# First branch's inverse multiplied into the scan's keys and output scores once per pair, two visits of TensorE per scan step instead of three, and a new order of the woven part

## Chip, cores and metric

The kernel runs on one core of one Trainium2 chip. The metric is device time in microseconds (us) of one execution; the times shown are of several executions of the same program. Names of engines: TensorE (PE in the profile, PEld its weight loads), VectorE (DVE), ScalarE (ACT), GpSimd (POOL), SyncE (SP, which issues most of the DMA).

## What is computed

One layer of a hybrid backbone over 256 latent tokens with a prefix of 256 context tokens, width 2048, in f32. After a modulated norm, one projection feeds two token mixers that run side by side, RWKV-7 time mixing (16 heads of 64) and a chunked gated DeltaNet (8 heads of 128), both in two directions, the context's final state being the start of the latent scan. A gated merge, an output projection and a SwiGLU FFN follow. The part that the change touches is the first mixer's recurrence:

```python
def rwkv7_scan(r, w, k, v, kk, bb, s0):
    def step(s, inp):
        r_t, w_t, k_t, v_t, kk_t, b_t = inp
        sa = jnp.einsum('bhij,bhj->bhi', s, kk_t)
        s = s * w_t[:, :, None, :] - sa[..., None] * b_t[:, :, None, :] + v_t[..., None] * k_t[:, :, None, :]
        return s, jnp.einsum('bhij,bhj->bhi', s, r_t)
    ...
    s_fin, y = lax.scan(step, s0, xs)
    return jnp.moveaxis(y, 0, 1), s_fin
...
out_a = [prefix_scan(rwkv7_scan, rwkv_dir_inputs(fa_c, d), rwkv_dir_inputs(fa, d), s0a, d == 1)
         for d in range(2)]
o_a = rwkv_readout(out_a[0][0] + out_a[1][0], fa, rw_r_k, rw_ln_w, rw_ln_b).astype(h.dtype)
```

## The kernel before

**Stages.** The program runs through a head (modulation, norm, the low-rank projections), a woven part (lines with the helper's line 145: both mixers and all remaining input projections), and then, in plain order, the merge (`pa`, `pb`), the output projection (`wout`), and the FFN (`wgu`, `wdn`). The woven part lies between about 134 and 1310 us of the profiled execution.

**The first mixer in chunks.** Heads go in 8 pairs, two heads of 64 on the two halves of the 128 partitions. The 512 tokens are cut into 8 chunks of 64 (4 of the context, 4 latent), in each of two directions. Per pair, `prepare` makes decayed keys, `grams` makes the chunk matrices (`LT`, the triangular matrix to invert; `LAl`/`LAc`, which carry state and values into the chunk; `Pm`, the output scores; `KB`, the keys token by token that carry the chunk's result into the state). `inverse` calls `invert`, which inverts 16 blocks of 64 and gives two views of the result, plain (`N_`, tile T0) and transposed (`Nt_`, tile Tx); `full` says whether both are made complete. `values` and `scan` follow. The second mixer's `head_inverse` uses the same `invert` with `full` set.

**A scan step.** `scan` takes 8 steps per pair, both directions and both heads at once. In a step TensorE is visited three times, each visit after a copy of the visit before:

1. `la` x `vx` into bank `ps` (four matmuls), then ScalarE copies the result to R1;
2. the inverse `Tt` x R1 into the other half of `ps` (four matmuls); with it go two identity matmuls that put the old state into bank `acc`, and in the latent steps four output matmuls; ScalarE then copies the result over the value rows of `vx`;
3. `KB` x `vx` onto `acc` (the new state), and in the latent steps `Pm` x `vx` (the output). VectorE scales the state by the chunk's decay and writes it into the next `vx`.

**What sets the order.** All woven work is written as generators. `Weave.run` goes through them before the kernel is built and fixes the order of instructions on each engine: it takes the piece that could start first by prices in `Lane` (`cost` of an instruction) and `LAT` (`hop` between engines, `turn` for a change of kind on TensorE, `grp` instructions at a time); among equals the lower rank given to `weave.add` goes first. On the chip each engine works strictly through its list and waits on semaphores. `products` issues the projection matmuls in split form, three f32r matmuls per weight block (`mm<-hxh,whi`, `mm<-hxl,whi`, `mm<-hxh,wlo`), with `cast` making `whi` on ScalarE and `wlo` on VectorE from loads that SyncE issues. 40 of these products are gate columns; `GATES_A` and `GATES_B` say how many of them are free to run beside which pair and which head. PSUM banks are shared out as `pab` (2 banks), `pib` (1), `psb` (2) and `mmb` (3).

Of the kernel before, what the change touches and what calls it, by code (L numbers as in the profile page):

```python
# [11 lines left out]
F32 = mybir.dt.float32  # L12
# [6 lines left out]
P = 128  # L19
# [91 lines left out]
class Lane:  # L111
# [5 lines left out]
    def __getattr__(self, name):  # L117

        def op(out, *a, **k):
# [8 lines left out]
            elif name == "matmul":  # L128
# [3 lines left out]
                elif rows <= 64 and m <= 64:  # L132
                    cost, kind = 0.026 if rows < 64 else max(0.06, 0.05 + 0.00015 * n), (rows, m)
                elif m <= 64:
                    cost, kind = 0.085 if m == 64 else 0.12, (rows, m)
                else:
                    cost = (0.0054 + 0.00167 * n) * (1.22 if rows == 96 else 1)
# [8 lines left out]
        return op  # L146

# [123 lines left out]
def emit(ctx: ExitStack, tc, A, out, dbg=None):  # L271
# [284 lines left out]
    def invert(pool, Lt, parts, nu, which, full, fill):  # L556
# [90 lines left out]
        yield [e.matmul(ps[src, 32 * i:32 * i + 32], qo[dst, i, :], Tx[dst, u, cd], start=True, stop=True)  # L647
               for i, h, u, src, dst, cs, cd in quads]
        for h in range(2):
            yield [out(Tx, d, h, ps, True) for d in range(2)]  # L650
        weave.release(pib)
        if full:
            ps = yield pib
            yield [e.matmul(ps[dst, 32 * i:32 * i + 32], Tx[dst, u, cd], qo[dst, i, :], start=True, stop=True)
                   for i, h, u, src, dst, cs, cd in quads]
            for h in range(2):
                yield [out(T0, d, h, ps, False) for d in range(2)]
            weave.release(pib)
# [59 lines left out]
    def lowrank():  # L718
# [17 lines left out]
        for p in range(NPAIR):  # L736
# [8 lines left out]
            for j in (0, 2, 1, 3):  # L745
                ps = yield psb
                yield e.matmul(ps, w[:96, 4 * (p % 2) + j], lin[:, j], start=True, stop=True)
                weave.add(2, lowrank_out(p, j, ps, out[j]))

    def prepare(p):  # L750
# [78 lines left out]
        if p + 1 < NPAIR:  # L829
            weave.add(10 * p + 13, prepare(p + 1))  # L830

    def grams(p, d):
# [4 lines left out]
        def m4(a, b, rows):  # L837
# [4 lines left out]
        yield [e.matmul(ps[h if src is ic else half[1 - j], 64 * c:64 * c + 64], src[h, T + 64 * c:T + 64 * c + 64],  # L842
                             lc[h, c, j, :], start=True, stop=True)
                    for c in range(4) for ps, src in ((p1, ic), (p2, kt)) for j, h in enumerate(half)]
# [7 lines left out]
        yield [e.matmul(ps[h if src is ic else half[1 - j], P * c:P * c + P], src[h, 64 * c:64 * c + 64], la[h, c, j, :],  # L852
                             start=True, stop=True) for c in range(4) for ps, src in ((p1, ic), (p2, kt)) for j, h in enumerate(half)]
# [23 lines left out]
    def inverse(p):  # L877
# [6 lines left out]
        _, o["Tt"], _ = yield from invert(rs, lambda h, u: LT[64 * h:64 * h + 64, u // 8, u % 8, :],  # L884
# [855 lines left out]
```

## Time and profile before

| what | us |
|---|---|
| median of 3 runs | 2293.3 |
| lowest, highest | 2292.33, 2308.79 |
| profiled execution: span from first to last instruction | 2286.3 |
| woven part in it | 134 to 1310 |
| of it the eight scans | 280 to 810 |
| merge and output projection | 1310 to 1560 |
| FFN | 1560 to 2286 |

The profiled execution gives a span only; its distance to the median of the runs (7.0 us) is what lies around the first and last instruction, plus the difference between runs. In the profile's rows a group reads: line, engine, operation, tiles out<-in, shapes, xcount | busy us, mean ns of one | idle time of the engine before them and what ended it. A window reads: stretch and its length, then busy us and (xcount) of PE, PEld, DVE, ACT, POOL, then the granted TensorE clock, the DMA share and GB/s. A wait reads: who waited <- for whom: us in total, times, the longest. A timeline row reads: start, us until the end of the merged instructions, engine, line, operation, tiles, forms, count. An f32 matmul of the program shows as two matmul instructions in the trace, an f32r matmul as one.

### The profile page before, as it was taken

Reading aid. Unit: us, or ns where it says so; the run is one execution under the profiler, and the core shown is the slowest. Engines: PE = TensorE matmul, PEld = TensorE weight load, DVE = VectorE, ACT = ScalarE, POOL = GpSimd, SP = SyncE. Lnnn points to the kernel's source line nnn. Section 1 sums busy time; section 2 is a strip of 40 time slices with the busy share of each in tenths; the row PEclk is TensorE's granted clock in tenths of the full one; section 3 lists DMA queues with packets and bytes.
Section 4 is the critical chain, followed back from the end, with each engine's and each line's share of the span. In section 5 each row is a group of like instructions: output and inputs, shape, how many; then the busy total and the mean of one; then the engine's idle time right before and its main releaser. Section 6 shows DMA issues by size and latency. Waiting matters only on the chain. (4 is left out here: it accounts for less than half of the span.)

```text
span 2286.3 us, 54678 instructions
## 1 busy us (share of the span) xinstructions
PE 2184.5 (96%) x22904; PEld 1925.0 (84%) x22904; DVE 1561.3 (68%) x3225; ACT 1056.6 (46%) x1922; POOL 110.3 (5%) x185
## 2 busy tenths in 40 slices
PE   7998999999999999999999989899999999999998
PEld 4766577777777788888888889889999999999997
DVE  3446588888877586899997668774656656444444
ACT  3245554544555554444453445444444444444443
POOL 0000000000000010111110040000000000000000
PEclk9999999999999999999999989999999999999999
DMA  9955643443443254555566696864777776566665
GB/s 384 407 148 170 187 113 89 117 106 99 106 101 100 87 180 141 162 163 165 167 188 216 232 350 230 283 207 142 237 238 236 236 233 214 186 185 192 186 189 162
DMA packets 231926, 430.76 MB, mean 188 GB/s; under 512 B 114944, under 2 KB 129152, under 8 KB 227328
## 3 DMA queue, kind: packets, MB, share of 16 engines
q1 hardware_dynamic: 203744, 350.72, 49.5%
q0 software_dynamic: 14112, 51.39, 7.1%
q10 hardware_dynamic: 13824, 25.17, 3.3%
q8 instruction: 179, 2.93, 0.5%
q14 instruction: 67, 0.55, 0.1%
HBM read 401.44 MB, written 25.77 MB: 187 GB/s over the span
## 5 line engine op out<-in xcount | busy, mean ns | idle before, releaser
L361 DVE TENSOR_TENSOR wlo<-wraw,whi 128x1024 fp32r<-128x1024 f32 x328 | 393.4, 1199 | 336.5 <-ACT whi L360 332.9
L360 ACT CAST whi<-wraw 128x1024 fp32r<-128x1024 f32 x328 | 337.5, 1029 | 469.2 <-PE mm L371 434.4
L145 PE MATMUL mm<-hxh,wlo 128*128 128x256 f32 (+1 forms) x1376 | 466.3, 339 | 7.3 <-DVE wlo L145 6.9
L145 PE MATMUL mm<-hxh,whi 128*128 128x256 f32 (+1 forms) x1376 | 464.7, 338 | 6.0 <-ACT whi L145 5.8
L145 PE MATMUL mm<-hxl,whi 128*128 128x256 f32 (+1 forms) x1376 | 462.2, 336 | 0.0
L372 PE MATMUL mm<-hfh,wlo 128*128 128x256 f32 x1344 | 374.9, 279 | 0.3 <-DVE wlo L361 0.3
L370 PE MATMUL mm<-hfh,whi 128*128 128x256 f32 x1344 | 374.9, 279 | 0.0
L371 PE MATMUL mm<-hfl,whi 128*128 128x256 f32 x1344 | 374.7, 279 | 0.0
L145 PEld LDWEIGHTS mm<-hxh,wlo 128*128 128x128 f32 x1376 | 262.4, 191 | 35.5 <-DVE wlo L145 10.0
L145 PEld LDWEIGHTS mm<-hxh,whi 128*128 128x128 f32 x1376 | 262.6, 191 | 33.3 <-ACT whi L145 7.2
L145 PEld LDWEIGHTS mm<-hxl,whi 128*128 128x128 f32 x1376 | 262.3, 191 | 25.2 <-issue 5.7
L145 DVE TENSOR_TENSOR wlo<-wraw,whi 128x512 fp32r<-128x512 f32 x344 | 236.1, 689 | 59.3 <-ACT whi L145 58.0
L372 PEld LDWEIGHTS mm<-hfh,wlo 128*128 128x128 f32 x1344 | 252.7, 188 | 0.5 <-DVE wlo L361 0.5
L370 PEld LDWEIGHTS mm<-hfh,whi 128*128 128x128 f32 x1344 | 252.8, 188 | 0.0
L371 PEld LDWEIGHTS mm<-hfl,whi 128*128 128x128 f32 x1344 | 252.7, 188 | 0.0
L145 ACT CAST whi<-wraw 128x512 fp32r<-128x512 f32 x344 | 205.0, 618 | 94.2 <-PE mm L145 56.9
L145 DVE TENSOR_TENSOR arena<-arena 128x512 f32<-128x512 f32 (+12 forms) x538 | 132.9, 248 | 28.2 <-DMA arena<-scr 13.5
L370 PE MATMUL mm<-za,whi 128*128 128x256 f32 x512 | 142.9, 279 | 0.0
L372 PE MATMUL mm<-za,wlo 128*128 128x256 f32 x512 | 142.7, 279 | 0.0
L371 PE MATMUL mm<-za,whi 128*128 128x256 f32 x512 | 142.7, 279 | 0.0
L370 PEld LDWEIGHTS mm<-za,whi 128*128 128x128 f32 x512 | 96.3, 188 | 0.0
L371 PEld LDWEIGHTS mm<-za,whi 128*128 128x128 f32 x512 | 96.3, 188 | 0.0
(318 smaller groups left out, 3907.5 us busy)
## 6 DMA issues: line engine op xcount, KB each, us to landing
wraw<-w SPq DMA_DIRECT2D x172, 512.0 KB, 4.1
wraw<-wgu SPq DMA_DIRECT2D x168, 512.0 KB, 4.5
aw<-ada_rest POOLq DMA_DIRECT2D x96, 512.0 KB, 5.2
aw<-ada_first SPq DMA_DIRECT2D x32, 1024.0 KB, 11.6
wraw<-wdn SPq DMA_DIRECT2D x64, 448.0 KB, 3.6
wraw<-wout SPq DMA_DIRECT2D x32, 512.0 KB, 4.8
aw<-ada_gt ACTq DMA_DIRECT2D x64, 256.0 KB, 4.8
wraw<-wdn SPq DMA_DIRECT2D x32, 512.0 KB, 3.6
```

The lines of the kernel that those rows point to most:

```text
L145: return Op(self, cost, lambda: getattr(self.engine, name)(out, *a, **k), kind)
L360: S.copy(hi[:, c, :M], raw[:, c, :M])
L361: V.tensor_sub(lo[:, c, :M], raw[:, c, :M], hi[:, c, :M].bitcast(F32))
L370: E.matmul(ps, hi, Xh[:, k, :n], start=first and i == 0, stop=False)
L371: E.matmul(ps, hi, Xl[:, k, :n], start=False, stop=False)
L372: E.matmul(ps, lo, Xh[:, k, :n], start=False, stop=last and i == len(wt) - 1)
```

## The change

The inverse no longer multiplies R1 in every step. After `invert`, `inverse` multiplies it once into the pair's `KB` (32 matmuls over both directions, 8 chunks and two heads) and into `Pm` (16 matmuls for the latent chunks), in one group on TensorE. ScalarE copies the two `pa` banks back over `KB` in four copies, VectorE the `pi` bank over `Pm` in one. For this `inverse` now waits for both `grams` of its pair, whose last outputs are `KB`, and takes both `pa` banks and the `pi` bank. In the step the second visit's inverse matmuls and the copy to R1 are gone; the identity and the output matmuls are issued directly behind the first visit's, and the copy over `vx` takes the first visit's result.

`invert` now always makes the plain view complete and the transposed one only with `full`: for the first mixer its last product of 32-blocks is replaced by one of the same count and size with the operands exchanged.

The order is set anew: all ranks come from a table, prices of small matmuls, `own` and `turn` are changed, groups that alternate between array quadrants are priced at half by `quad` (which has no effect but on the order), and the gate products are shared out anew (21 beside the pairs and 19 beside the heads, as before).

```diff
-GATES_A, GATES_B = ((6, 3, 0, 2, 3, 3, 1, 3), (3, 0, 0, 0, 0, 2, 6, 8))
-LAT = dict(dma=2.4, hop=0.3, own=0.1, grp=32, crank=-1, cg=4, turn=0.13)
+GATES_A, GATES_B = (6, 2, 1, 4, 0, 1, 4, 3), (2, 3, 0, 0, 2, 2, 9, 1)
...
+LAT = dict(dma=2.4, hop=0.300, own=0.092, grp=32, cg=4, turn=0.170)
...
-                    cost, kind = 0.026 if rows < 64 else max(0.06, 0.05 + 0.00015 * n), (rows, m)
+                    cost, kind = (0.01 + 0.00037 * n if rows < 64 else 0.01 + 0.00075 * n), (rows, m)
...
+def quad(ops):
+    for o in ops:
+        o.cost *= 0.5
+    return ops
...
     def inverse(p):
...
-        _, o["Tt"], _ = yield from invert(rs, lambda h, u: LT[64 * h:64 * h + 64, u // 8, u % 8, :],
-                                          lambda h, d: [(0, LT[64 * h:64 * h + 64, d])], 16, p % 2, False, g)
+        N, _, _ = yield from invert(rs, lambda h, u: LT[64 * h:64 * h + 64, u // 8, u % 8, :],
+                                    lambda h, d: [(0, LT[64 * h:64 * h + 64, d])], 16, p % 2, False, g)
+        for d in range(2):
+            yield "grams", p, d
+        KB, Pm = o["KB"], o["Pm"]
+        p0, p1 = yield pab, pab
+        pm = yield pib
+        ops = []
+        pairs = [(d, c) for d in range(2) for c in range(8)]
+        for i, (d, c) in enumerate(pairs):
+            ops += [e.matmul((p0, p1)[d][half[1 - j], 64 * c:64 * c + 64], N(j, 8 * d + c), KB[half[j], d, c, j, :],
+                             start=True, stop=True) for j in range(2)]
+            if i % 2:
+                dm, m = divmod(i // 2, 4)
+                ops += [e.matmul(pm[half[j], T * dm + 64 * m:T * dm + 64 * m + 64], N(j, 8 * dm + m), Pm[half[j], dm, m, :],
+                                 start=True, stop=True) for j in range(2)]
+        yield quad(ops)
+        for d, ps in enumerate((p0, p1)):
+            yield [s.copy(KB[half[j], d, :, j, :], c3(ps[half[1 - j]])) for j in range(2)]
+            weave.release(pab)
+        yield v.tensor_copy(Pm.rearrange("p d c k -> p (d c k)"), pm)
+        weave.release(pib)
         weave.ready("inverse", p)
...
     def scan(p):
...
             yield ops
-            R1 = rs.tile([P, 2, 64], F32, tag="R1", name="R1")
-            yield s.copy(R1.rearrange("p d t -> p (d t)"), ps[:, 0:P])
-            yield [e.matmul(ps[h, P + 64 * d:P + 64 * d + 64], Tt(j, 8 * d + cs_[d]), R1[h, d, :], start=True, stop=True)
-                   for d, j, h in dh]
...
-                yield s.copy(vx[h, both, j, :], c3(ps[h, P:2 * P]))
+                yield s.copy(vx[h, both, j, :], c3(ps[h, 0:P]))
...
         for p in range(NPAIR):
             for d in range(2):
-                weave.add(10 * p + 2, grams(p, d))
-            weave.add(10 * p + 1, inverse(p))
-            weave.add(10 * p + 4, values(p))
-            weave.add(10 * p, scan(p))
+                weave.add(10 * p + RANK['grams'], grams(p, d))
+            weave.add(10 * p + RANK['inverse'], inverse(p))
+            weave.add(10 * p + RANK['values'], values(p))
+            weave.add(10 * p + RANK['scan'], scan(p))
```

In the table the scan has -54, the inverse -58, the cast of a product's weights -94 and the pair's `prepare` 53, each with 10 more per pair but the cast; before, the scan had 0, the inverse 1 and `prepare` 3 in the same way, and the cast -1.

More of the change, by code (lines that the diff above doesn't have):

```diff
@@ L646, in invert @@
         yield v.tensor_copy(qo, ps[:, 0:32 * h2].rearrange("p (i c) -> p i c", c=32))
[L647 removed]
+        if full:
+            yield [e.matmul(ps[src, 32 * i:32 * i + 32], qo[dst, i, :], Tx[dst, u, cd], start=True, stop=True)
+                   for i, h, u, src, dst, cs, cd in quads]
+            for h in range(2):
+                yield [out(Tx, d, h, ps, True) for d in range(2)]
+            weave.release(pib)
+            ps = yield pib
+        yield [e.matmul(ps[dst, 32 * i:32 * i + 32], Tx[dst, u, cd], qo[dst, i, :], start=True, stop=True)
                for i, h, u, src, dst, cs, cd in quads]
         for h in range(2):
[L650 removed]
+            yield [out(T0, d, h, ps, False) for d in range(2)]
         weave.release(pib)
[L652 to L658, printed above, removed]
         return N_, Nt_, Tx
@@ L851, in grams @@
         p1, p2 = yield pab, pab
-        yield [e.matmul(ps[h if src is ic else half[1 - j], P * c:P * c + P], src[h, 64 * c:64 * c + 64], la[h, c, j, :],
-                             start=True, stop=True) for c in range(4) for ps, src in ((p1, ic), (p2, kt)) for j, h in enumerate(half)]
+        yield quad([e.matmul(ps[h if src is ic else half[1 - j], P * c:P * c + P], src[h, 64 * c:64 * c + 64], la[h, c, j, :],
+                             start=True, stop=True) for c in range(4) for ps, src in ((p1, ic), (p2, kt)) for j, h in enumerate(half)])
         pv = p1.rearrange("p (c t) -> p c t", t=P)
@@ L920, in scan @@
             yield "grams", p, d
-        LAl, LAc, KB, Pm, Tt, et = [o["la", d] for d in range(2)], [o["lc", d] for d in range(2)], o["KB"], o["Pm"], o["Tt"], o["et"]
+        LAl, LAc, KB, Pm, et = [o["la", d] for d in range(2)], [o["lc", d] for d in range(2)], o["KB"], o["Pm"], o["et"]
         Y = rs.tile([P, 4, 64], F32, tag="Y", name="Y")
```

30 lines of the change are left out of this document (16 added, 14 removed).

## Prediction

> **What bounds the kernel now.** I read the page's busy rows first, then busy time by stage, then TensorE's waits, then single visits in the timeline.
>
> ```profile
> PE 2184.5 (96%) x22904; PEld 1925.0 (84%) x22904; DVE 1561.3 (68%) x3225; ACT 1056.6 (46%) x1922; POOL 110.3 (5%) x185
> ...
> PEclk9999999999999999999999989999999999999999
> 134.00:280.00 146.00, 128.84 (x1108) 93.01 (x1109) 88.91 (x197) 83.79 (x148) 3.64 (x8) 0.95 0.59 176
> 280.00:810.00 530.00, 516.54 (x7562) 396.58 (x7561) 420.61 (x1057) 266.83 (x666) 18.77 (x48) 1.00 0.39 102
> 810.00:1310.00 500.00, 482.52 (x4983) 420.24 (x4983) 419.33 (x1068) 236.48 (x475) 50.41 (x78) 0.99 0.60 181
> ```
>
> TensorE is busy 96% of the span. The change lives in the woven part: its head (134 to 280 us), the eight scans (280 to 810) and the second branch (810 to 1310). In the scans TensorE works 516.5 of 530 us at full granted clock, VectorE 421, ScalarE 267. TensorE sets this stage's length, and the split products (projection matmuls, names beginning mm<-hx) fill the time between scan steps. Their number does not change. So the change is worth what it does to the sum of TensorE's work, plus what the new order does to its waits. Those are small:
>
> ```profile
> PE mm L145 <- DVE wlo L145: 6.9, 10, 1.8
> PE pa L145 <- ACT arena L145: 6.2, 6, 2.1
> PE pi L145 <- DVE arena L145: 6.1, 7, 2.3
> PE mm L145 <- ACT whi L145: 5.8, 5, 1.9
> PE pi L145 <- issue: 4.0, 6, 1.3
> PE s L145 <- DVE Vn L145: 3.9, 5, 2.7
> PE s L145 <- ACT lo L145: 3.7, 3, 2.0
> PE pa L145 <- issue: 2.6, 3, 1.3
> ...
> PE s L145 <- ACT VX L145: 1.1, 3, 0.5
> ```
>
> These are all of TensorE's waits from 134 to 1310 us, the longest first. By the windows the idle time is 17.2 + 13.5 + 17.5 = 48 us. Only 1.1 us of it is the scan waiting for its own copies. So a shorter chain of dependences by itself frees almost nothing; what counts is instructions and visits.
>
> **What goes: the second visit.**
>
> ```profile
> 508.67 0.28 PE L145 MATMUL mm<-hxh,wlo 128*128 128x256 f32 x1
> 508.79 0.28 PE L145 MATMUL mm<-hxh,whi 128*128 128x256 f32 x1
> 508.90 0.28 PE L145 MATMUL mm<-hxl,whi 128*128 128x256 f32 x1
> 509.11 0.45 PE L145 MATMUL s<-VX,KB 128*64 128x64 f32 x8
> 509.50 0.38 PE L145 MATMUL mm<-hxh,wlo 128*128 128x256 f32 x1
> ...
> 512.81 0.45 PE L145 MATMUL s<-R,Tx 64*64 64x64 f32 x8
> 513.09 0.39 PE L145 MATMUL s<-VX,C 64*64 64x128 f32 x4
> 513.41 0.50 PE L145 MATMUL mm<-hxl,whi 128*128 128x512 f32 x1
> ```
>
> Durations overlap, so I go from start to start. (The trace shows each f32 matmul as two instructions: x8 is four in the program.) The inverse's eight take 513.09 - 512.81 = 0.28 us. There are 8 pairs x 8 steps = 64 such groups: 64 x 0.28 = **17.9 us removed**.
>
> Turning to small work and back costs too. Split products of 256 columns follow each other after 0.115 us (508.67, 508.79, 508.90), but the small group starts 0.21 us after the last of them: 0.095 lost. It then takes 0.39 us to the next product, while eight at 0.28/8 = 0.035 each need 0.28: 0.11 lost. That is 0.2 us a visit. Counted in the built order, the woven part has 461 unbroken runs of small work before and 434 after: 27 x 0.2 = **5.4 us removed**. It is not 64, since part of the old second visits already stood next to other small work, and others are divided anew.
>
> The step on TensorE, one in the first half of a scan, before (R is the tile that the code names R1):
>
> ```order
> L145 MATMUL s<-VX,LAc 64x64 x4
> L145 MATMUL mm<-hxh,whi 128x512
> L145 MATMUL mm<-hxl,whi 128x512
> L145 MATMUL mm<-hxh,wlo 128x512
> L145 MATMUL mm<-hxh,whi 128x512
> L145 MATMUL s<-R_3886,Tx 64x64 x4
> L145 MATMUL s<-VX,C 64x128 x2
> L145 MATMUL mm<-hxl,whi 128x512
> L145 MATMUL pa<-C,arena 128x128 x4
> L145 MATMUL mm<-hxh,wlo 128x512
> L145 MATMUL s<-VX,KB 64x64 x4
> ```
>
> And a step of the same half now:
>
> ```order
> L146 MATMUL s<-VX,LAc 64x64 x4
> L146 MATMUL s<-VX,C 64x128 x2
> L146 MATMUL mm<-hxh,wlo 128x256
> L146 MATMUL mm<-hxh,whi 128x256
> L146 MATMUL mm<-hxl,whi 128x256
> L146 MATMUL mm<-hxh,wlo 128x256
> L146 MATMUL mm<-hxh,whi 128x256
> L146 MATMUL mm<-hxl,whi 128x256
> L146 MATMUL mm<-hxh,wlo 128x256
> L146 MATMUL mm<-hxh,whi 128x256
> L146 MATMUL s<-VX,KB 64x64 x4
> ```
>
> The state's identity matmul (s<-VX,C) has moved up beside the first product, and one stretch of products now covers the step's copy where two did.
>
> **What comes: the multiply.** Per pair 32 + 16 = 48 matmuls, so 96 instructions in the trace, 768 in all. Two groups of the same size (64x64, moving 64 columns) are the nearest rows:
>
> ```profile
> 502.89 1.06 PE L145 MATMUL pa<-LAc,arena 64*64 64x64 f32 x32
> ...
> 503.88 0.39 PE L145 MATMUL mm<-hxh,whi 128*128 128x256 f32 x1
> 932.10 0.68 PE L145 MATMUL pi<-T,LT 64*64 64x64 f32 x16
> 932.71 0.50 PE L145 MATMUL mm<-hxh,whi 128*128 128x512 f32 x1
> ```
>
> Less the 0.11 of the way out, the first is (0.99 - 0.11)/32 = 27.5 ns an instruction, spread over all four quadrants of the array; the second (0.61 - 0.11)/16 = 31 ns over two. The multiply alternates two quadrants for KB and puts in the other two for Pm: between them, 30 ns. 768 x 0.030 = **23.0 us added**, with ends 21.1 and 23.8. [...]
>
> Long runs of small instructions sometimes stop for a reason that the trace doesn't show:
>
> ```profile
> 610.62 0.34 PE L145 MATMUL pa<-LAc,arena 64*64 64x64 f32 x7
> 612.28 0.62 PE L145 MATMUL pa<-LAc,arena 64*64 64x64 f32 x25 [1.32 <-issue]
> ```
>
> Nine such waits make 6.6 us in the woven part. If each of the eight multiplies met one of 1.3 us, it would be 10.4 us; if none, 0. I take 1, since nine fell on all the small runs there are. [...]
>
> **The other engines.**
>
> ```profile
> L145 ACT COPY R<-s 128x128 f32<-128x128 f32 x64 | 16.9, 265 | 62.6 <-PE s L145 61.9
> L145 ACT COPY KB<-pa 64x256 f32<-64x256 f32 x128 | 46.9, 366 | 14.4 <-PE pa L145 12.2 <-PE mm L145 0.4
> L145 ACT COPY VX<-s 64x128 f32<-64x128 f32 x128 | 33.2, 259 | 50.5 <-PE s L145 48.8
> L145 DVE TENSOR_TENSOR LAl<-pa,C 64x512 f32<-64x512 f32 x32 | 22.0, 688 | 0.8
> L145 PEld LDWEIGHTS s<-R,Tx 64*64 64x64 f32 x512 | 20.1, 133 | 15.6 <-issue 7.6 <-ACT R L145 3.0 <-ACT whi L145 1.6
> L145 PE MATMUL s<-R,Tx 64*64 64x64 f32 x512 | 28.4, 229 | 0.0
> L145 DVE COPY Y<-s x16: 281/292/293, 308.5 to 794.5; 128x128 f32<-128x128 f32 x16
> ```
>
> ScalarE loses 16.9 us of R copies and gets 32 copies of 64x512. From 64x128 to 64x256 a copy grows by 0.107 us, so 64x512 is 0.366 + 2 x 0.107 = 0.58, at most the 0.69 that VectorE takes: 18.6 to 22 us. It is 50% busy there: nothing on the path. VectorE gets 8 copies of 128x512, 8 x 0.69 = 5.5 us, in a stage with 109 us free. Weight loads waited 3.0 us for R, but the matmuls' own idle time is 0.0: other work hid it. I take -1, ends -3 and 0. The first visit now needs the accumulator bank that the output copy (Y<-s, 0.29 us) still reads in three steps of a pair: at most 24 x 0.29 = 7 us, I take 1, since VectorE does this copy while the four state matmuls run. The swapped last product of the 32-blocks costs the same count and size: nothing. No load is added; the loads of products only come in another order on SyncE's queue.
>
> Sum: -17.9 - 5.4 + 23.0 + 1 - 1 + 1 = **+0.7 us**. TensorE's work is even, from -9 to +18 with all ends at once.
>
> **The order set anew.** Ranks, prices and the placing of the gate products (21 beside the scans and 19 later, both times) change throughout, so the 48 us of idle time are dealt anew. The head stands almost unchanged, and its 17 us stay. In the other 31 us I expect a fifth less, 6 us: each step asks for one covered wait less, so 64 stretches of products (four in the first order shown) can stand at other waits. This is a choice; the rows bound it by -31 and by nothing above. Together -5 us: span 2281, and as the median lies 7.0 above the profiled span of 2286.3, 2288.
>
> **The rivals.**
>
> *Faster.* The freed stretches close two thirds of the 31 us (-21) and the multiply runs near its lower end (-2): 2271. For it: the waits for VectorE and for tiles of the inverse are single ones up to 2.3 us, which a better order can cover. Against: VectorE is 84% busy in the second branch (419 of 500), so its lateness there is not only order. Chance 0.2, half of it over 1%.
>
> *Slower.* The multiply holds both pa banks and the pi bank until ScalarE has emptied the pa pair and VectorE the pi bank. ScalarE now has, at the start of the fourth pair's scan:
>
> ```order
> L146 ACTIVATE arena<-mm,om 128x512
> L146 CAST whi<-wraw 128x512
> L146 COPY KB<-pa 64x8x64 x4
> L146 CAST whi<-wraw 128x512 x2
> L146 COPY VX<-s 64x2x64 x2
> ```
>
> and at the start of the same scan before:
>
> ```order
> L145 COPY KB<-pa 64x4x64 x2
> L145 COPY R_5790<-s 128x128
> L145 COPY KB<-pa 64x4x64 x2
> L145 ACTIVATE arena<-mm,om 128x512
> L145 CAST whi<-wraw 128x512
> ```
>
> Where copies of KB, of R and casts took turns, the four copies now stand in one block of 4 x 0.58 = 2.3 to 2.75 us, and the casts that the next products need stand behind it, as does the scan's first copy. The products of one weight tile (8 blocks x 3 x 0.115 = 2.8 us) cover that just once; where the cast before is late, TensorE waits the whole block, and the pi bank's 0.69 after it: 8 x (2.3 to 3.4) = 18 to 27 us, 2307 to 2316 and with the upper end of the issue waits over 2320. Against: before, TensorE waits only 5.8 us for whi in the whole woven part. Chance 0.15, half of it over 1%.
>
> *Not what it says.* The merged visits could be pulled apart on the chip by the accumulator bank, so that three visits remain in effect: back come 5.4 and the 7 of that bank, 2300. Chance 0.07.
>
> **How the numbers follow.** The forecast, work even and waits slightly fewer, has 0.58: 2280 to 2298. The range takes in most of both rivals: 2268 to 2308. One per cent (23 us) is what I count as told apart from no change. Faster 0.10 and slower 0.08 are the halves of the two rivals; the rest is within.
>
> **What would show it.** In the changed profile: s<-R,Tx and R<-s gone; pa<-KB and pi<-Pm x768 together at 27 to 31 ns from start to start; TensorE still 97% busy between 280 and 810; the scans' stage within 10 us of 530; waits of mm for ACT whi not above 10 us. Wrong if TensorE's idle time in the woven part leaves 35 to 60 us, or if the multiply takes over 3.5 us a pair.

## The result and the profile after

| | before | after |
|---|---|---|
| median of 12 runs each, us | 2298.62 | 2294.44 |
| lowest, highest | 2292.33, 2308.79 | 2287.66, 2304.96 |
| ratio after / before, 95% interval | | 0.9993 [0.9976, 1.0009] |
| profiled span | 2286.3 | 2292.4 |
| woven part, first woven matmul to first product of the output projection (mm<-oah) | 1177.9 | 1177.3 |

No change that can be measured. (The ratio on record is formed from all runs and is not the quotient of the two medians, 0.9982; its interval is -5.5 to +2.1 us.) The two profiled spans differ by 6 us the other way, but not in the woven part: behind it, where both kernels run the same code, the profile before took 974.2 us and the one after 980.8. Over the later executions in which no woven work stands behind that point it took 975 to 983 us, so the profile before lies at the low end. The woven part itself repeats well: two profiled executions of the same kernel differ in it by 0.2 us (after and e1) and by 2.2 us (e7 and e13).

The changed kernel's page, its busy row and the DMA queue q8, named "instruction":

```profile
PE 2189.3 (96%) x23160; PEld 1934.4 (84%) x23160; DVE 1570.3 (68%) x3233; ACT 1065.8 (46%) x1891; POOL 116.4 (5%) x185
...
q8 instruction: 181, 2.97, 0.5%
```

The same three stages (busy us of PE, PEld, DVE, ACT, POOL, then the granted clock, DMA share and GB/s):

```profile
134.00:280.00 146.00, 127.49 (x1182) 92.36 (x1183) 84.19 (x189) 84.07 (x145) 3.50 (x6) 0.94 0.57 169
280.00:810.00 530.00, 513.51 (x7706) 401.12 (x7704) 423.38 (x1058) 271.44 (x634) 17.71 (x42) 0.98 0.39 105
810.00:1310.00 500.00, 485.04 (x5025) 419.61 (x5023) 427.81 (x1086) 240.91 (x481) 57.15 (x84) 1.00 0.59 180
```

TensorE still sets the pace: 513.5 of 530 us in the scans, where it was 516.5. Its idle time in the three windows is 18.5 + 16.5 + 15.0 = 50 us, where it was 48. But the granted clock in the scans has gone from 1.00 to 0.98. And the waits of TensorE in the woven part have changed places:

```profile
PE pi L146 <- issue: 12.5, 8, 2.2
PE mm L146 <- ACT whi L146: 7.5, 5, 2.0
PE pa L146 <- ACT arena L146: 5.6, 9, 0.9
PE mm L146 <- DVE wlo L146: 5.3, 8, 1.8
PE s L146 <- ACT TF L146: 3.5, 1, 3.5
PE s L146 <- DMA wraw<-lora: 3.2, 2, 2.1
PE pi L146 <- DVE arena L146: 2.2, 4, 1.7
...
PE pa L146 <- issue: 1.2, 2, 0.9
...
PE s L146 <- ACT VX L146: 0.3, 1, 0.3
```

At the top now stands "issue": TensorE waits although no engine and no DMA of data that the trace shows keeps it. It was 4.0 + 2.6 = 6.6 us, it is 12.5 + 1.2 = 13.7. All other waits together (gaps over 50 ns, up to the first mm<-oah) fell from 42.8 to 37.5.

Where the new waits stand, and what they do to the clock, the timeline of the fourth pair shows:

```profile
483.17 0.40 PE L146 MATMUL mm<-hxh,wlo 128*128 128x512 f32 x1
483.49 1.26 PE L146 MATMUL pi<-arena 32*32 32x16 f32 x128
484.68 1.22 PE L146 MATMUL pa<-LAl,arena 64*64 64x128 f32 x32
485.83 0.50 PE L146 MATMUL mm<-hxh,whi 128*128 128x512 f32 x1
486.17 0.39 PE L146 MATMUL mm<-hxl,whi 128*128 128x512 f32 x1
486.40 0.40 PE L146 MATMUL mm<-hxh,wlo 128*128 128x512 f32 x1
486.73 0.29 PE L146 MATMUL pi<-arena,Tx 32*32 32x16 f32 x11
488.89 1.16 PE L146 MATMUL pi<-arena,Tx 32*32 32x16 f32 x117 [1.87 <-issue]
...
490.55 0.39 PE L146 MATMUL mm<-hxh,wlo 128*128 128x512 f32 x1
490.79 0.49 PE L146 MATMUL mm<-hxh,whi 128*128 128x512 f32 x1
491.07 0.63 PE L146 MATMUL mm<-hxl,whi 128*128 128x512 f32 x1
491.50 0.63 PE L146 MATMUL mm<-hxh,wlo 128*128 128x512 f32 x1
491.93 0.63 PE L146 MATMUL mm<-hxh,whi 128*128 128x512 f32 x1
```

The two groups of 128 tiny matmuls with which `invert` starts stand almost next to each other; only one `pa` group and three products lie between. In the second the engine stops for 1.87 us with all its operands ready, as far as the trace shows. Two microseconds later the products follow each other after 0.43 us instead of 0.23. The windows around it show the granted clock at 0.51 there:

```profile
487.50:490.90 3.40, 2.01 (x121) 1.85 (x121) 2.21 (x6) 0.00 (x0) 0.00 (x0) 1.00 0.41 137
490.90:494.30 3.40, 3.40 (x12) 2.71 (x11) 3.35 (x8) 1.66 (x6) 0.00 (x0) 0.51 0.02 5
494.30:497.70 3.40, 3.40 (x78) 2.68 (x78) 2.48 (x7) 2.26 (x6) 0.00 (x0) 0.99 0.28 77
```

After a window with 2.01 us of work in 3.4, the clock is granted at 0.51 for the next 3.4 us, about half. In the scans this happens five times (the clock's records begin at 422.7, 490.9, 559.2, 627.5 and 695.7 us), each time within about 2 us of the end of an issue wait of 1.6 us or more; before, it happened once there (371.5).

The same pair's first two groups in the kernel before, for comparison. Nine products lie between them, and no issue wait falls here:

```profile
479.25 1.32 PE L145 MATMUL pi<-arena 32*32 32x16 f32 x128
480.49 0.44 PE L145 MATMUL pa<-C,arena 128*128 128x128 f32 x2
480.69 0.48 PE L145 MATMUL mm<-hxh,wlo 128*128 128x512 f32 x1
...
482.64 0.40 PE L145 MATMUL mm<-hxl,whi 128*128 128x512 f32 x1
484.10 1.26 PE L145 MATMUL pi<-arena,Tx 32*32 32x16 f32 x128 [1.06 <-DVE arena L145]
```

The difference between the two kernels is one of degree. The two groups with all that stands between them take, as a mean over the eight pairs and without the issue waits, 2.4 us for every 256 of TensorE's instructions before and 2.1 after. (A matmul and its weight load are two instructions; the page of after has 23160 of each.)

**What the issue waits are.** Number TensorE's instructions through the whole program, a weight load and its matmul as two, the semaphore instructions with them. Every issue wait of over 0.1 us between 134 and 1312 us, before, after and in all later runs listed below, is at number 193 or 194 modulo 256. The queue q8 moves packets of 16,384 bytes, 181 in after for 2 x 23160 = 46,320 matmuls and weight loads, one for about every 256. The waits end 1.16 to 1.46 us after such a packet has landed in after, 1.31 to 1.55 us in before. From the trace of after, us:

```
packet from - to       TensorE waits from - to     landing to resumption
418.40 - 419.36        419.17 - 420.82             1.46
486.68 - 487.64        487.02 - 488.89             1.25
556.74 - 557.69        557.28 - 559.14             1.45
624.86 - 626.27        625.93 - 627.58             1.31
692.71 - 693.66        693.01 - 694.89             1.23
```

I read these figures as TensorE having run out of instructions and waiting for the next block of 256. How fast the blocks are used up (issue waits not counted), and which have a wait, in the woven part:

```
                              before        after
blocks                        108           110
used up in under 3.15 us      3             11
  of them with a wait, us     2, 2.1        9, 12.7
3.15 to 4 us                  11            4
  of them with a wait, us     6, 4.0        1, 0.9
4 to 5.5 us                   7             11
  of them with a wait, us     1, 0.5        0
over 5.5 us                   87            84
  of them with a wait         0             0
```

In these two executions none of the 171 blocks that lasted over 5.5 us had a wait, and 11 of the 14 that were used up in under 3.15 us had one. Over all 15 profiled executions a wait followed 47 of 63 blocks that lasted under 3 us, 38 of 99 of 3 to 4 us, 18 of 167 of 4 to 5.5 us, and 3 of some 1290 longer ones. One tiny group of 128 in the trace is 256 instructions with its weight loads, a whole block, and takes 1.2 us (483.49 to 484.68 above).

### The profile page after: what moved, and what is told of

The parts are those of the page before. It is cut to its first block, busy times and chain, and to the rows that moved or that the text cites. A ratio compares the mean times of both kernels' runs of the same rounds, so it can differ in the third digit from the quotient of the medians.

```text
span 2292.4 us, 55178 instructions
## 1 busy us (share of the span) xinstructions
PE 2189.3 (96%) x23160; PEld 1934.4 (84%) x23160; DVE 1570.3 (68%) x3233; ACT 1065.8 (46%) x1891; POOL 116.4 (5%) x185
## 3 DMA queue, kind: packets, MB, share of 16 engines
q1 hardware_dynamic: 203744, 350.72, 49.4%
## 4 chain that ended last, share of the span: by engine, by line
PE 72%; DVE 11%; DMA 7%; issue 5%; ACT 4%; SPq 1%; POOL 0%; ACTq 0%; DVEq 0%; POOLq 0%
PE mm L146 19%; PE mm L377 13%; PE mm L379 12%; PE mm L378 12%; PE s L146 6%; PE pa L146 5%; DVE arena L146 3%; DVE wlo L146 2%; PE pi L146 2%; DMA wr<-wgu 1%; PE mm L465 1%; DVE aw L146 1%; DMA wraw<-pa 1%; DMA aw<-ada_rest 1%; DVE wlo L368 1%
## 5 line engine op out<-in xcount | busy, mean ns | idle before, releaser
L146 DVE TENSOR_TENSOR arena<-arena 128x28 f32<-128x28 f32 (+13 forms) x538 | 131.3, 247 | 22.7 <-DMA arena<-scr 8.0
L146 DVE SCALAR_TENSOR_TENSOR aw<-aw,ck 128x512 f32<-128x512 f32 x120 | 90.0, 759 | 10.6 <-DMA aw<-ada_rest 10.4
L378 PEld LDWEIGHTS mm<-za,whi 128*128 128x128 f32 x512 | 96.3, 188 | 0.0
```

Source lines behind the costliest of these rows:

```text
L146: return Op(self, cost, lambda: getattr(self.engine, name)(out, *a, **k), kind)
L378: E.matmul(ps, hi, Xl[:, k, :n], start=False, stop=False)
```

## The experiments

The time that the clock loses is the length of its records below 1 times what is missing; it is an upper bound, since TensorE isn't always at work in them. The first columns are from one profiled execution of each kernel, woven part only, but for the second, which goes on to the first product of the FFN (mm<-hfh); then come the medians of all runs. The second column is there because in e2, e4 and e9 to e12 the last 58 to 180 small matmuls of the second mixer (7 to 11 us) stand behind the first mm<-oah, so their woven part is too short by them; in all others none does. Each ratio is to runs of before made beside it, whose medians were 2295.1 us (e1 to e4), 2292.2 (e5 to e8), 2293.5 (e9 to e12) and 2293.3 (e13), and not to the first row.

```
                     woven   to FFN   issue  other   clock   blocks under  runs: median,  ratio to before
                     us      us       waits  waits   lost    3.15 us       us (number)
before               1177.9  1398.1    6.6   42.8    15.3     3            2298.62 (12)
after                1177.3  1397.3   13.7   37.5    18.7    11            2294.44 (12)   0.9993 [0.9976, 1.0009]
e1_after_again       1177.5  1401.5   15.6   34.0    22.1    10            2293.47 (10)   1.0003 [0.9981, 1.0025]
e2_spread            1160.9  1387.1    4.8   40.2    17.0     3            2283.17 (10)   0.9953 [0.9934, 0.9973]
e3_edit_alone        1181.8  1407.2   10.2   45.5    20.4     5            2296.88 (10)   1.0018 [1.0001, 1.0035]
e4_order_alone       1179.9  1408.3    6.1   48.3    23.8     2            2302.21 (10)   1.0040 [1.0022, 1.0058]
e5_pad               1183.6  1404.2   17.8   35.6    27.2    12            2296.30 (1)
e6_multiply_twice    1206.0  1431.2   23.2   36.4    28.9    20            2323.48 (1)
e7_no_second         1173.3  1396.5    2.6   47.5    23.8     2            2294.71 (1)
e8_before_spread     1214.0  1437.7    0.6   62.9    35.7     3            2328.62 (4)    1.0152 [1.0125, 1.0180]
e9_spread_1us        1166.4  1395.6    6.3   41.2    23.6     3            2285.97 (7)    0.9959 [0.9936, 0.9981]
e10_spread_3us       1166.5  1392.8    1.9   43.7    20.4     2            2288.14 (10)   0.9972 [0.9952, 0.9991]
e11_spread_multiply  1161.9  1390.8    1.6   40.7    17.0     3            2284.16 (7)    0.9946 [0.9922, 0.9971]
e12_spread_16        1170.0  1400.9    1.8   44.1    20.4     0            2293.86 (10)   0.9995 [0.9979, 1.0011]
e13_no_second_again  1171.1  1392.9    5.4   47.9    17.0     2            2283.24 (10)   0.9963 [0.9939, 0.9986]
```

### The changed kernel again, and its dense groups spread (e1, e2)

The first is the changed kernel as it is. The second takes apart the two long lists of 32x16 products in `invert` and edits nothing else:

```diff
+def spread(ops, n=32, pause=2.0):
+    for i in range(0, len(ops), n):
+        if i:
+            yield pause
+        yield ops[i:i + n]
...
-        yield [e.matmul(pv[r, 0, u], Lt(h, u)[...], T0[r, u, ...], start=True, stop=True) for h, u, b, r in fours]
+        yield from spread([e.matmul(pv[r, 0, u], Lt(h, u)[...], T0[r, u, ...], start=True, stop=True) for h, u, b, r in fours])
...
-        yield [e.matmul(pv[r, 1, u], Tx[r, u, b:b + 32], Qm[r, u, :], start=True, stop=True) for h, u, b, r in fours]
+        yield from spread([e.matmul(pv[r, 1, u], Tx[r, u, b:b + 32], Qm[r, u, :], start=True, stop=True) for h, u, b, r in fours])
```

The pause is a planned one: it only tells the planner that the next half may start later, so that it puts products between the halves. The planner then places all other woven work anew as well.

> The changed kernel itself, beside the next three on one chip. Both theories: woven part (first to last woven product) 1177 us within 3, TensorE's waits put down to issue 13 to 14 us in some ten pieces, all at the same instruction number modulo 256; ratio to before 0.998 to 1.001.

> The two long runs of 64 small matmuls at the start of each inverse are handed out as 32 and 32 with a planned pause of 2 us between; same work. Fetch theory (TensorE's list arrives in blocks of 256 instructions, and it waits where it uses up a block in under about 5 us): issue waits fall from 13.7 to under 4 us and the woven part shortens by about 10 us to 1167; ratio to before about 0.995. Rival (idle time is only passed on from one cause to another): issue waits fall but others rise by as much, woven part 1175 to 1180, ratio 0.999. Second rival (issue waits belong to the small matmuls themselves, not to the stream): they stay at 10 us or more.

The changed kernel repeats itself: woven part 1177.5, issue waits 15.6. Spread, the woven part is 16.4 us shorter than after, but 9.3 us of small groups have moved behind its end; to the first product of the FFN it is 10.2 us (14.4 against e1), and the medians of the runs side by side differ by 10.3. TensorE's issue waits in it:

```profile
PE pi L146 <- issue: 3.9, 3, 1.8
PE mm L146 <- issue: 0.7, 1, 0.7
PE pa L146 <- issue: 0.2, 1, 0.2
```

The stretch in which a group now stands; products of 128x256 on both sides, and half as many tiny matmuls at once:

```profile
497.51 0.28 PE L146 MATMUL mm<-hxh,whi 128*128 128x256 f32 x1
497.62 0.28 PE L146 MATMUL mm<-hxl,whi 128*128 128x256 f32 x1
497.83 0.73 PE L146 MATMUL pi<-arena 32*32 32x16 f32 x64
498.49 0.66 PE L146 MATMUL pa<-C,arena 128*128 128x128 f32 x4
498.90 0.36 PE L146 MATMUL mm<-hxh,wlo 128*128 128x256 f32 x1
```

Eleven blocks used up in under 3.15 us became three, and issue waits of 13.7 us became 4.8 (under 4 was expected). The waits were not passed on: the others rose by 2.7 us only. So the 8.9 us of issue waits that are gone are most of what was gained; the clock, to the first product of the FFN, loses up to 5 us less. The number of runs of small work is no part of it: counted that far it is 439 in after and 437 here (the 419 of the expectations stop at the first mm<-oah).

### The edit alone, the order alone (e3, e4)

e3 is the algorithm of after with the ranks, prices and gate counts of before; e4 is the new order table with the three-visit algorithm of before. The diffs are the two halves of the change's own diff.

> The multiply and the two visits with all ranks, prices and gate shares of before. The built order has 411 runs of small work (461 before, 434 in the changed kernel). By the sum of work: -17.9 for the inverse's products, -10 for 50 visits, +23 for the multiply, -5 in all, and issue waits between 5 and 14 us: woven part 1170 to 1178, ratio 0.996 to 1.000. Rival (the edit needs the new order, since old prices put the new groups badly): other waits rise by 10 us or more, woven part over 1183, ratio over 1.003.

> The ranks, prices and gate shares of the changed kernel with the three visits of before; 448 runs of small work. If the new order brings what I forecast (other waits 6 us fewer) and the issue waits do not grow: 13 visits give -2.6, together -8: woven part 1169, ratio 0.996. Fetch theory: the dense runs stand close together in the new order too, so issue waits are again 10 us or more and the woven part is 1173 to 1179. Rival (the order has no gain): other waits stay at 44 us and the woven part is over 1176 with issue waits under 8.

Neither half is a gain. The edit in the old order has 412 runs of small work, fewer than after, and gives that back in waits and clock: 55.7 us of idle time where before had 49.4, 27.2 of it for VectorE (24.6), 10.2 for issue (6.6), and up to 5 us more lost to the clock. Its 1181.8 us lie between the two things expected. The new order without the edit is 0.4% slower than before, with waits for ScalarE up from 17.7 to 24.8 us. What was expected of it by the fetch theory, issue waits of 10 us or more, did not come: it has 6.1, and two blocks under 3.15 us. The third expectation fits, an order without a gain. So the dense places of after come neither from the new table of ranks and prices alone (two such blocks) nor from the edit alone (five), but from both together (eleven). Each is fitted to the other, so what the edit is worth can't be read from before's order, nor the order's from before's algorithm.

### The blocks shifted (e5)

32 more small matmuls, 128 instructions, in the head of the program; their result is not used.

```diff
+            if e == 0:
+                for _ in range(32):
+                    E.matmul(pt[0:32, P:2 * P], ckr[:, 0].rearrange("p a b -> p (a b)"), rows, start=True, stop=True)
```

> The changed kernel with 32 more small matmuls early in the head (64 matmuls and 64 weight loads in the trace, 128 instructions; their result is not used): the woven part has the same order, moved by 128 in the count of TensorE's instructions. Fetch theory: every issue wait is again at number 193 or 194 modulo 256 of the list, so each stands 128 instructions away from where it stood in the woven work; their sum changes by several us (4 to 18). Rival (the waits belong to the place in the work, say the first products of the inverse): they stay at the same matmuls, now at 65 modulo 256, with about 13.7 us.

All 13 issue waits of the woven part are again at 193 or 194 modulo 256, and so 128 instructions earlier in the work than in after. This tells a block's edge from anything in the instructions themselves: the same instructions that waited in after now run through, others wait. The dense runs are still there, and with them the waits: 17.8 us, the longest 4.07, and the clock loses up to 27.2.

### The multiply twice (e6)

```diff
-        yield quad(ops)
+        quad(ops)
+        again = [Op(o.lane, 0.0, o.call, o.kind) for o in ops]
+        yield [o for i in range(0, len(ops), 6) for o in ops[i:i + 6] + again[i:i + 6]]
```

> The changed kernel with every matmul of the multiply issued twice (the second at no price to the planner, so that the order stays); 768 more instructions in the trace. My price of 30 ns each: work +23 us, and more issue waits (0 to 10): woven part 1200 to 1210. [...] Rival (it is hidden between other work): under +8.

The woven part is 28.7 us longer. An undisturbed pair's multiply goes from 2.01 to 3.88 us for twice 96 instructions, which is 1.87 / 96 = 19.5 ns each; all eight together go from 16.7 to 35.0 us, 3 us of it issue waits that now fall in them. The issue waits rise by 9.5 us in all and the clock loses up to 10 more. So the added instructions cost 8 x 1.87 = 15 us of their own and nearly as much again in issue waits and clock. That the 1206 us lie in the stretch expected first, 1200 to 1210, is luck: the price of 30 ns was too high, and the waits made up for it.

### The old second visit taken out of the kernel before (e7, e13)

R copies and inverse matmuls are not issued, everything else keeps its place:

```diff
+def held(op):
+    op.call = lambda: None
+    return op
...
-            yield s.copy(R1.rearrange("p d t -> p (d t)"), ps[:, 0:P])
-            yield [e.matmul(ps[h, P + 64 * d:P + 64 * d + 64], Tt(j, 8 * d + cs_[d]), R1[h, d, :], start=True, stop=True)
+            yield held(s.copy(R1.rearrange("p d t -> p (d t)"), ps[:, 0:P]))
+            yield [held(e.matmul(ps[h, P + 64 * d:P + 64 * d + 64], Tt(j, 8 * d + cs_[d]), R1[h, d, :], start=True, stop=True))
```

> The kernel before with the copy to R1 and the inverse's products in the scan left out and everything else in its place, so that the scan uses values that the inverse was not applied to: 457 of the 461 runs of small work stay. My price: -17.9 us for 512 instructions and -1 for four visits; waits may move a little: woven part 1157 to 1162. Rival (the wait for R is worth more than its instructions, as the chain of three copies sets the scan): woven part under 1150. Rival (products lie beside other work): over 1167.

> e7 again with rounds: the kernel before without the copy to R1 and the inverse's products in the scan, order held. One execution showed the time of before (2294.7) at a clock of 0.981 where before has 0.984. Theory (TensorE's work sets the time, and e7's loss was the clock after waits that a too early TensorE meets in an order made for more work): the mean clock is again under 0.983, ratio 0.996 to 1.000. Rival (chance: that execution was a slow one): clock 0.984 and ratio 0.992 to 0.994, as 18 us less work would give. Rival (TensorE's work in the scan does not matter at all): clock 0.984 and ratio 1.000.

The single run of e7 showed no gain (2294.71 against 2292.22); ten runs showed 0.9963, 10.0 us less than the 2293.27 of the runs beside them. The single run was no measure of a difference of this size. The expected 17.9 us came back by half; the woven part of 1173.3 and 1171.1 us is what e7's last expectation had (over 1167). Of e13's expectations none fits whole: the ratio is that of the theory, but the mean clock, 0.984, is that of before. From start to start, the scan's small groups took 109.3 us in before and 97.0 here, so 12.3 of it is seen on TensorE; the identity matmuls stay where they were and still need their own way in and out. Waits grew by 3.8 us. In after, where these matmuls have moved to the first visit, the same groups take 91.6: 17.7 less.

### The spreading in the kernel before (e8), a miss

The same edit as e2 in the old algorithm and its order.

> The kernel before with its inverse's long runs handed out as 32 and 32 with 2 us between, 462 runs of small work. Fetch theory: its issue waits of 6.6 us fall under 3; woven part 1172 to 1176, ratio 0.996 to 0.999. Rival (idle time is passed on): 1178, ratio 1.000.

The issue waits went, as expected, and the kernel became 1.5% slower. TensorE's waits, the first three and the issue row:

```profile
PE pi L145 <- DVE T L145: 7.8, 4, 3.0
PE mm L145 <- DVE wlo L145: 6.3, 8, 1.8
PE pa L145 <- ACT arena L145: 5.4, 9, 2.1
...
PE pi L145 <- issue: 0.6, 2, 0.3
```

and its second branch:

```profile
810.00:1310.00 500.00, 464.38 (x4629) 390.29 (x4628) 402.78 (x1039) 223.24 (x448) 53.95 (x81) 0.95 0.53 160
```

The idle time rose by 14 us and the clock lost up to 20 more (0.95 here, where before had 0.99): together at most 34 of the 36 us. Its last scan ends at 834.6 us instead of 807.0. One could think that the planned pauses lengthen the inverse and so move later work to where fewer products are left to cover it. But e2's last scan ends nearly as much later (837.3 instead of 814.2 in after), and e2 is faster. So why the same edit loses in this order and gains in the new one stays open.

### Variants of the spreading (e9 to e12)

A shorter pause, a longer one, the multiply taken in halves as well, and parts of 16 with the short pause (the differing lines side by side, each with its run):

```diff
-def spread(ops, n=32, pause=2.0):
+def spread(ops, n=32, pause=1.0):      # e9
+def spread(ops, n=32, pause=3.5):      # e10
+def spread(ops, n=16, pause=1.0):      # e12
...
-        yield quad(ops)
+        yield from spread(quad(ops), 24)      # e11, pause 2.0
```

> As e2, with 1 us between the parts of 32 in place of 2 (427 runs of small work; e2 has 419). Fetch theory, by dose: 128 instructions in 0.7 us and 1 us of products make a block of 256 last about 3.4 us where 5 are needed, so issue waits lie between those of e2 (4.8) and of the changed kernel (13.7 to 15.6), and so does the mean granted clock (0.9859 and 0.9805); ratio to before 0.997 to 0.999. Rival (what gained in e2 was a lucky order of the rest): ratio and issue waits do not go together.

> As e2, with 3.5 us between the parts (416 runs of small work). Fetch theory: a block of 256 now lasts over 5 us in the inverse; issue waits under 4 us, clock 0.985 or more. The inverse ends later by 2 x 1.5 us in each pair; if the scans wait for it, other waits rise by up to 24 us: ratio 0.995 if they do not, up to 1.003 if they do.

> As e2, and the multiply too is handed out in two halves with 2 us between (432 runs of small work). The one long wait of e2 that stood in a multiply (1.8 us) goes; 8 more visits cost 1.6 us, and the banks are held 2 us longer per pair. Fetch theory: issue waits under 4 us, ratio 0.994 to 0.997. If holding the banks costs, other waits rise and the ratio is over 0.998.

> As e2, in parts of 16 with 1 us between (463 runs of small work, 44 more than e2). Fetch theory and price of a visit: issue waits under 4 us and clock as in e2, but 44 x 0.2 = 9 us more work: ratio 0.998 to 1.000. Rival (visits cost nothing of their own): ratio 0.995.

Three of the four are faster than the kernel before, and their medians lie below both medians of after; their intervals overlap with e2's, so they aren't told apart. e11 has the lowest ratio, 0.9946, and 1.6 us of issue waits in two places. e9 and e10 missed in part: the first, with 6.3 us of issue waits, was expected at 0.997 to 0.999 and has 0.9959; the second has only 1.9 us but a mean clock of 0.983 (0.985 or more was expected) and 0.9972. So among the variants the time does not follow the issue waits alone, and that a part of e2's gain is the order that came with it can't be ruled out.

e12 leaves no block under 3.15 us and 1.8 us of issue waits, and wins nothing. To the first product of the FFN it has 47 more runs of small work than e2 (484 against 437; 463 and 419 up to the first mm<-oah) and is 13.8 us longer. Issue waits are 3.0 us fewer in it, other waits up to there 3.7 more, and the clock loses up to 3.4 more; that leaves 9.7 to 13.1 us for the 47 visits, 0.21 to 0.28 each, near the prediction's 0.2. So here removing the waits paid only where it didn't cut the small work into more pieces.

## Why the forecast was right or wrong, step by step

The time, 2294.4 us, lay in the range and in the forecast's 2280 to 2298, but the gain of 5 us did not come in the part that changed: it is 0.6 us shorter in after and 0.4 in e1. (The runs alone don't rule 5 us out, by the interval above.) That the sum came out even is luck in good part: one term was too high by 6 us and another too low by as much. From start to start on TensorE, in the woven part, the change is this:

```
the scan's small groups                             109.3 ->  91.6    -17.7
other small groups that write a tile s              103.9 -> 101.4     -2.5
turn from products to small work                     48.6 ->  47.5     -1.1
pa and pi groups                                    187.7 -> 205.5    +17.8
   of it the multiply, 8 pairs                                        +16.7 (no issue wait in it)
   issue waits, all in other groups                                    +7.0
   the rest                                                           -5.9
products, over 0.234 us (512 columns) and 0.117     71.2 ->  74.2      +3.0
sum                                                                    -0.5
```

**TensorE sets the length: right.** The stage of the scans has 513.5 busy of 530 us, and e6 lengthens the part by more than the time of the instructions that it adds.

**The second visit, -17.9 and -5.4: right for the most part.** s<-R,Tx and R<-s are gone. The scan's groups are 17.7 us shorter and the turns 1.1, together -18.8 against -23.3. e3, the edit in the old order, has -15.0 in the scan's groups and e4, the order alone, +1.1: so it is the edit's. e13, which leaves the identity and output matmuls where they were, has -12.3.

**The multiply, +23.0: mis-sized by 6.** In the trace of after, the first and the last rows of one:

```profile
433.46 0.39 PE L146 MATMUL mm<-hxh,wlo 128*128 128x512 f32 x1
433.78 0.27 PE L146 MATMUL pa<-KB,arena 64*64 64x64 f32 x2
...
435.63 0.23 PE L146 MATMUL pa<-KB,arena 64*64 64x64 f32 x2
435.79 0.39 PE L146 MATMUL mm<-hxh,whi 128*128 128x256 f32 x1
```

It takes 435.79 - 433.78 = 2.01 us, and so in seven of the eight pairs (the other, 2.61, stops for a copy of KB in its middle); less 0.11 to 0.15 for the way out that is 1.86 to 1.90 / 96 = about 19.5 ns an instruction. Both the prediction's ends (27.5 and 31, from groups in other quadrant patterns) were too high; a pair stays far under the 3.5 us that were set as a sign of being wrong.

**The issue waits, +1 with ends 0 and 10.4: the step that failed.** It said "I take 1, since nine fell on all the small runs there are" and asked how many of the eight multiplies would meet one. They met none; the one multiply that stops in its middle waits for a copy:

```profile
364.59 0.27 PE L146 MATMUL pa<-KB,arena 64*64 64x64 f32 x2 [0.38 <-ACT KB L146]
```

The waits fell on work that the edit doesn't touch, eight of ten in the inverse's two dense groups, the other two in the `pa` group that now stands between them in most pairs. The two groups stood near each other before, too; with the edit and the new order together all this is so close that blocks of 256 were used up in 1.6 to 3.1 us. Measured: +7.0 in one execution, +9.0 in the other (e1). The term was priced by number of groups; the waits went by how fast a block was used up: 12.7 of the 13.7 us in after belong to blocks used up in under 3.15 us. And they had a consequence that was no term at all: behind the six of 1.6 us and more in after the clock is halved for 3.4 us (granted 0.51 from 490.9 to 494.3). By the clock's records that costs at most 3.4 us more in after than before (6.8 in e1), which is of the size of the +3.0 in the products' row, and the mean granted clock of the runs is 0.981 in after where it was 0.984 before and 0.986 in e2. That the dense groups bring the waits is shown by e2, which edits these two lists alone: 8.9 of the 13.7 us of waits go, and it is 10.3 us faster than after beside it. That the clock makes up the +3.0 is argued from the sizes.

**ScalarE's copies, nothing on the path: right.**

```profile
L146 ACT COPY KB<-pa x160: 364/368/587, 204.9 to 774.8; 64x256 f32<-64x256 f32 x128, 64x512 f32<-64x512 f32 x32
```

The large copies take up to 0.587 us, as estimated (0.58). The casts behind them made no queue: mm waits 7.5 us for ACT whi, under the 10 that were set, and s 0.3 us for VX. So the slower rival did not happen. Nor did the third one: no row shows the first visit waiting for VectorE's output copy.

**Fewer other waits, -6: right in size.** 42.8 to 37.5 is -5.3, all of it waits for VectorE (24.6 to 13.8) less what those for ScalarE and DMA rose by. The order without the edit does not bring it (48.3 in e4). The faster rival, with two thirds of them closed, did not happen.

With the terms as measured: -18.8 (second visit and turns) - 2.5 (the other groups of s) + 16.7 (the multiply) + 7.0 (issue waits) - 5.9 (the rest of pa and pi, of a size with the other waits that went) + 3.0 (products, most likely the clock) = -0.5. The issue waits, and by these sizes the clock, took what the cheaper multiply and the better order had won.

**Three workings of the prediction do not come out.** None of them moved the forecast by much. With all ends at their lowest its sum is -17.9 - 5.4 + 21.1 + 0 - 3 + 0 = -5.2, not -9; no run shows the other 3.8, and the multiply measured at 16.7 us lies 4.4 below the lower end of 21.1 that was taken for it. The range up to 2308 takes in only the lower edge of the slower rival, 2307 to 2316. And of the 7.0 us between span and median before, little lies around the first and last instruction: wherever both figures of one execution are on record they differ by 1.7 to 3.3 us. The execution profiled before was a short one.

**What stays open.** Why the waits crowd at blocks that last under 4 us (85 of 162, against 18 of 167 of 4 to 5.5 us) was not tried: the trace of after shows about 1 us of transfer (median 0.99) and 1.16 to 1.46 from landing to resumption, and not when a packet is asked for. Of the 17.9 us, e13's woven part, 6.8 us shorter, misses 11: the scan's groups save 5.6 less, the turns cost 2.8 more and the pa and pi groups 3.6 more, with 3.8 us of waits among them; what makes them so isn't settled. Nor is how much of e2's gain the clock has, or why the same spreading loses 1.5% in the order of before.

## What to carry to other kernels

Here small matmuls cost more than their own time where they stood close together: in after, nine of the 11 blocks of 256 instructions, weight loads included, that TensorE used up in under 3.15 us had a wait, 12.7 us in all, and none of the 84 that lasted over 5.5 us had one. To see whether another kernel has such places, count the instructions that TensorE uses up in stretches of a few us, and where they crowd try wide products between them, but without adding runs of small work (the 47 more in e12 cost 9.7 to 13.1 us), and measure it: here this gained 0.5% in one order (e2) and lost 1.5% in another (e8). In these profiles the sign was "issue" waits that lie a whole number of 256 instructions apart, and the clock's column just behind the longer ones showed their second price (0.51 for 3.4 us in after). A change that sets an order anew is to be searched for such places even in work that its diff doesn't touch, and an edit and the order made for it can't be priced apart.

## What the runs showed of the hardware that was not expected

- TensorE ran out of instructions, as I read the packets and the waits: blocks of 256 that lasted over 5.5 us brought one wait each in three of 15 executions, 0.4 us at most; those under 3.15 us had 12.7 us of waits in after, single ones up to 2.2 us, and 4.1 in e5.
- In after the clock was halved for 3.4 us behind all six issue waits of 1.6 to 2.2 us; the 3.4 us ahead of the halving held 1.4 to 2.05 us of TensorE's work. A stretch with as little work did not always bring it: the one from 1108.8 to 1112.2 us held 1.75 us, and the clock stayed full behind it. The granted clock was 0.51 from 490.9 to 494.3 us; the clock's records behind those six waits last 3.41 us each, and the starts of two of them, 422.7 and 490.9, lie 68.2 us apart, 20 times as much.
- f32 matmuls of 64x64 by 64 columns that change quadrants went at 19.5 ns an instruction (the multiply in after and e6), and 128 of 32x16 at 1.2 us / 128 = about 9 ns (483.49 to 484.68 in after).
